# Other pauses of TensorE's side threads in a two-layer RWKV7 and latent-attention block, and a higher scheduler priority for its attention scores

## The chip, the cores and the metric

The kernel runs on one core of one Trainium2 chip. The metric is the device time of one execution in microseconds (us). Engines are named as in the profile: PE is TensorE, DVE is VectorE, ACT is ScalarE, POOL is GpSimd, SP is SyncE.

## The reference, cut to what matters

One block with two layers works on 256 tokens of width 2048. Each layer mixes tokens in two ways from one input projection, a linear-attention recurrence (RWKV7, 16 heads of 64) and a causal softmax attention with compressed keys and queries (MLA, 8 heads), then projects both together with `w_out`. A memory cross-attention and a feed-forward part (2048 to 8192 and back) follow.

```python
def rwkv7_scan(r, decay, k, v, kk, a):
    def step(state, inp):
        r_t, w_t, k_t, v_t, kk_t, b_t = inp
        sa = jnp.einsum('bhvk,bhk->bhv', state, -kk_t)
        state = (state * w_t[:, :, None, :]
                 + sa[..., :, None] * b_t[:, :, None, :]
                 + v_t[..., :, None] * k_t[:, :, None, :])
        return state, jnp.einsum('bhvk,bhk->bhv', state, r_t)
...
    if v_first is None:
        v_first = v
    else:
        vr = token_shift(vres_cols, mu_vres)
        v = v + (v_first - v) * jax.nn.sigmoid(v0 + vr @ v_up)
...
def causal_block_attention(qn, qr, kn, kr, v):
...
        s = (jnp.einsum('bqhd,bkhd->bhqk', qn[:, q0:q1], kn[:, :q1])
             + jnp.einsum('bqhr,bkr->bhqk', qr[:, q0:q1], kr[:, :q1])).astype(jnp.float32) * scale
...
        p = jax.nn.softmax(s, axis=-1).astype(v.dtype)
        outs.append(jnp.einsum('bhqk,bkhd->bqhd', p, v[:, :q1]))
```

In layer 1 the values `v` are blended with those of layer 0 (`v_first`); in layer 0 they are not. That is why one edit below depends on the layer.

## The kernel before, in words

**The main line.** All large products (called gemms here) run on PE. A weight tile of 128x1024 is loaded by SP (512 KB), rounded on ACT to a high part `wh` (L291), and the remainder `wl` is made on DVE by a subtraction (L292). Each product is done three times, as wh with the high part of the activations, wl with the high part and wh with the low part, and these PE rows all carry the line L243 (transposes L248).

**The side threads.** The small chains of each layer are Python generators, called fibers: `f_inner` (the RWKV chunk products of a group of 8 heads), `f_v` (the values), `f_qr` (rotary queries), `f_lane` (three attention heads), `f_out` (end of the recurrence) and others. Each layer has two groups, g0 and g1. PE's order is written out by the program itself (`tc.manual_schedule` for PE alone, L1522): after every step of a gemm the main line calls `poll()` (L185), which lets every fiber run whose due time has passed. The clock for this is a model, `self.clk`, which each matmul advances by an estimate. `yield x` in a fiber means: come back when this clock has moved on by x times 1.1 (`LAT`, L164). So a longer pause puts more gemm products between two steps of a fiber, and everything later in that fiber stands later in PE's order. Nothing of this clock exists on the chip: there PE takes its rows in the order written and waits for operands and buffers.

The other four engines are ordered by the Tile scheduler from program order and priorities; `high_priority(offset=300)` makes it treat the instructions inside as if they stood 300 places earlier.

**PSUM.** The fibers share four banks, given out in turn by `xps()` (tiles `x`); the gemms have four more (tiles `g`). A bank is free again only when the engine that empties it has done so.

**Where the change acts.** `f_inner` multiplies four chunks: each takes two banks and 16 small matmuls (L720, rows `x<-AR,BK`), then DVE multiplies by a mask out of the two banks (L723, `W<-x,C`, two rows), ACT copies the diagonal blocks (L725), and the fiber pauses at L728. After the fourth chunk come the bonus products (L743, `x<-prod,C`) and three rounds of transposes (L751, `x<-Id,BK`, copied by ACT at L752). The operands AR and BK are made on DVE (L688 to L696), the `prod` tiles at L701. `f_v` waits at L836 until the values `vT` are there (token shift: `yp` L496, `yd` on POOL L501, `vT` L504). In layer 1 it then blends in `v_first` (POOL's DMA at L842 and products at L843 and L844, DVE's addition L845) and pauses 6.2 (L849); then it transposes the values in two rounds of four (L854, `x<-Id,vT`, copied by ACT at L857). `f_lane` computes the scores of a head, takes the masked row maximum on DVE (L1145, L1147), the exponential on ACT (L1150) and the division by the sum on DVE (L1152, L1155), pauses 9.6, and transposes (`x<-Id,pr`). The results of the query and key gemms leave PSUM through ACT (`kn` L1109, `qn` L1115) and DVE (`vv` L1112). `f_out` ends the recurrence: normalised outputs `oc` (L953) are transposed (`x<-Id,oc`) and gated (`x<-gl,gup`), DVE makes `yo` (L964, L966), ACT its high part `oh` (L967), DVE the low part `ol` (L968), and the `w_out` gemm reads `oh` and `ol`. That gemm's rows with these operands are named `g<-wh,oh`, those with the attention's operands `mh` and `ml`. The recurrence's own chain on DVE, a long row of small pairs (L798, L800), runs beside all this.

Of the kernel before, what the change touches and what calls it, by code (L numbers as in the profile page):

```python
# [11 lines left out]
AF = mybir.ActivationFunctionType  # L12
ALU = mybir.AluOpType
# [9 lines left out]
NEG = -3.0e38  # L23
# [110 lines left out]
class K:  # L134
# [571 lines left out]
    def f_inner(self, l, g, R, prods):  # L706


        nc = self.nc
# [4 lines left out]
        for c in range(4):  # L714
            W = self.t4("W", [128, 8, 128])
            pw = [self.xps().rearrange("p (h t) -> p h t", h=4) for _ in range(2)]
            for i in range(4):
                for q in range(2):
                    rows = slice(64 * q, 64 * q + 64)
                    self.mm(pw[q][:, i, :], BK[i // 2][rows, i % 2, c].rearrange("p a b -> p (a b)"),  # L720
                            AR[i // 2][rows, i % 2, c].rearrange("p a b -> p (a b)"), True, True)
            for q in range(2):
                nc.vector.tensor_tensor(out=W[:, 4 * q : 4 * q + 4, :], in0=pw[q], in1=mw, op=ALU.mult)  # L723
            for b in range(2):
                nc.scalar.copy(out=G[b * 32 : b * 32 + 32, :, c * 8 : c * 8 + 8].rearrange("p t i -> p i t"),  # L725
                               in_=W[b * 32 : b * 32 + 32, :, b * 32 : b * 32 + 32])
            Ws.append(W)
            yield (0.1, 0.1)[g]  # L728
        N = self.t4("N", [128, 32, 32])
        nc.vector.transpose(out=N[:64].rearrange("p a b -> p (a b)"), in_=G[:64].rearrange("p a b -> p (a b)"))  # L730
        nc.vector.tensor_copy(out=N[64:], in_=N[:64])
# [15 lines left out]
        for c in range(3):  # L747
            tok = self.t2("tok", [128, 8, 64])
            ps = self.xps().rearrange("p (i t) -> p i t", i=4)
# [16 lines left out]
        for h in range(2):  # L766
            nc.gpsimd.memset(UT[64 * h + 32 : 64 * h + 64, :, :, 0:32], 0.0)
            for b in range(2):
                nc.scalar.copy(out=UT[64 * h + 32 * b : 64 * h + 32 * b + 32, :, :, 32 * b : 32 * b + 32],
                               in_=Ud[32 * b : 32 * b + 32].rearrange("p (c g j) t -> p c g j t", c=4, g=2)[:, :, h])  # L770
        yield (1.2, 1.2)[g]
        for half in range(2):
# [4 lines left out]
            for h in range(2):  # L777
                nc.scalar.copy(out=UT[64 * h : 64 * h + 32, 2 * half : 2 * half + 2, :, 32:64],
                               in_=p2[0:32].rearrange("p (c g j) t -> p c g j t", c=2, g=2)[:, :, h])
# [35 lines left out]
    def f_v(self, l, g, sm, R):  # L815
# [3 lines left out]
        if l:  # L819
# [5 lines left out]
            for b in range(2):  # L825
# [8 lines left out]
                sgs.append(sg)  # L834
                yield (1.0, 1.0)[g]
        yield ("vT", l, g)  # L836
        vT = R["vT"]
        for b in range(2):
            bs = slice(2 * b, 2 * b + 2)
# [282 lines left out]
    def f_lane(self, l, heads, M):  # L1122
        nc = self.nc
        sc = float(192.0) ** -0.5
        am = self.c("amask")
        yield ("qr", l)
        mh, ml = M["m"]
        for h in heads:
            g, i = h // 4, h % 4
            yield ("proj", l, g)  # L1130
            kn, vv, qn = M["k"][g]
            qrT, krz = M["qrT"], M["krz"]
            ps = self.xps()
            pr = self.t2("pr", [128, 384])
            mx, nm, sm, ri = (self.sm(s, [128, 2]) for s in ("mx", "nm", "sum", "ri"))
            for t in range(2):
                n = 128 * (t + 1)
                o = ps[:, t * 128 : t * 128 + n]
                ts = slice(t * 128, (t + 1) * 128)
                self.mm(o, qn[:, i, ts], kn[:, i, :n], True, False)  # L1140
                self.mm(o, qrT[:, h // 2, ts], krz[:, h % 2, :n], False, True)
            for t in range(2):
                n = 128 * (t + 1)
                o = ps[:, t * 128 : t * 128 + n]
                nc.vector.tensor_tensor_reduce(out=o, in0=o, in1=am[:, t * 128 : t * 128 + n], scale=1.0, scalar=NEG,  # L1145
                                               op0=ALU.add, op1=ALU.max, accum_out=mx[:, t : t + 1])
            nc.vector.tensor_scalar(out=nm, in0=mx, scalar1=-sc, scalar2=None, op0=ALU.mult)  # L1147
            for t in range(2):
                n = 128 * (t + 1)
                nc.scalar.activation(out=pr[:, t * 128 : t * 128 + n], in_=ps[:, t * 128 : t * 128 + n], func=AF.Exp,  # L1150
                                     scale=sc, bias=nm[:, t : t + 1], accum_out=sm[:, t : t + 1])
            nc.vector.reciprocal(out=ri, in_=sm)  # L1152
            for t in range(2):
                n = 128 * (t + 1)
                nc.vector.tensor_scalar(out=pr[:, t * 128 : t * 128 + n], in0=pr[:, t * 128 : t * 128 + n], scalar1=ri[:, t : t + 1], scalar2=None, op0=ALU.mult)  # L1155
            yield 9.6
            pt = self.xps()
            for b in range(3):
                self.tr(pt[:, b * 128 : (b + 1) * 128], pr[:, b * 128 : (b + 1) * 128])
            prT = self.t2("prT", [128, 384])  # L1160
            nc.scalar.copy(out=prT, in_=pt[:, :384])
            yield 2.0
            po = self.xps()
            vs = slice(i * 128, (i + 1) * 128)
            self.mm(po[:, 0:256], vv[:, 0, vs], prT[:, 0:256], True, False)
            self.mm(po[:, 128:256], vv[:, 1, vs], prT[:, 256:384], False, True)
            o = mh[h // 4][:, h % 4, :]
            nc.scalar.copy(out=o, in_=po[:, :256])
            nc.vector.tensor_tensor(out=ml[h // 4][:, h % 4, :], in0=po[:, :256], in1=o.bitcast(F32), op=ALU.subtract)
            self.fire(("mla", l, h), 1.5)  # L1170
            yield 0.1
# [366 lines left out]
```

## Time and profile before

| what | value |
|---|---|
| median of 3 runs | 2571.5 us (2571.23 to 2571.56) |
| profiled execution | 2572.03 us |
| its span | 2570.3 us |
| mean granted TensorE clock | 0.99 |
| PE busy | 2504.9 us (97%), so 65.4 us idle |
| DVE busy | 1655.6 us (64%) |
| ACT busy | 1211.0 us (47%) |
| POOL busy | 457.8 us (18%) |

Times in the profile count from the start of the span. A timeline row gives the start, the busy time, the engine, the line, the operation, the tiles (output, then inputs), shapes, and `x` with the number of instructions merged in it; in brackets stands how long the engine was idle before it and which instruction ended that. A row of the windows gives, for a stretch of time, the busy time and number of instructions of each engine, the clock granted to PE (PEclk, 1.00 is full), the share of DMA engines in use, and GB/s. A row of the waits gives the waiting instruction, the one that ended the waits, and how much in all, how often, and the longest.

### The profile page before, as it was taken

What the parts mean: (1) busy time and instruction counts of PE and PEld (TensorE: products, weight loads), DVE (VectorE), ACT (ScalarE), POOL (GpSimd) and SP (SyncE); (2) the same over time, 40 slices, a digit from 0 to 9 for tenths busy, and PEclk for the clock granted to TensorE, in tenths of its full rate; (3) what the DMA queues carried; (4) which work ended last, traced back from release to release, by engine and by line L of the source; (5) the groups of instructions that cost most, each with busy time, mean ns of one, the idle gap of its engine ahead of it and who ended that gap; (6) DMA issues with size and microseconds to landing.
All of it is one profiled execution on the core that took longest, in us unless ns stands there. A gap on an engine that the chain in (4) does not pass through costs nothing.

```text
span 2570.3 us, 39517 instructions
## 1 busy us (share of the span) xinstructions
PE 2504.9 (97%) x15538; PEld 2176.2 (85%) x15538; DVE 1655.6 (64%) x2245; ACT 1211.0 (47%) x1740; POOL 457.8 (18%) x609
## 2 busy tenths in 40 slices
PE   8999999999999999999999998999999999999998
PEld 7989888978888888888788987889788888888886
DVE  4776876676565566566757778656755655665665
ACT  5454555554444444444454544545544443444443
POOL 3323425221000000001124244202200000000010
PEclk9999999999999999999999999999999999999999
DMA  6555356746666666666654544565466566666664
GB/s 228 151 154 139 121 167 204 229 135 183 193 189 189 193 189 189 189 192 206 199 168 135 155 126 122 163 226 186 137 186 193 190 183 197 190 188 190 194 205 132
DMA packets 257163, 456.53 MB, mean 178 GB/s; under 512 B 25588, under 2 KB 58740, under 8 KB 256976
## 3 DMA queue, kind: packets, MB, share of 16 engines
q1 hardware_dynamic: 247600, 422.79, 53.1%
q0 software_dynamic: 9376, 31.21, 3.9%
q8 instruction: 122, 2.00, 0.3%
q14 instruction: 65, 0.53, 0.1%
HBM read 444.50 MB, written 9.44 MB: 177 GB/s over the span
## 4 chain that ended last, share of the span: by engine, by line
PE 86%; DVE 6%; POOL 2%; issue 2%; ACT 1%; DMA 1%; SPq 0%; DVEq 0%; POOLq 0%; ACTq 0%
PE g L243 52%; PE x L243 33%; DVE wl L292 2%; PE x L248 2%; DMA raw<-in_w_in_dram 1%; ACT wh L291 1%; DVE fs L798 1%; DVE T L800 0%; DVE h L485 0%; ACT junk L396 0%; DMA raw<-in_w_ff_dram 0%; DMA vf<-vfirst 0%; DVE uf L424 0%; POOL yd L501 0%; POOL rsn L647 0%
## 5 line engine op out<-in xcount | busy, mean ns | idle before, releaser
L292 DVE TENSOR_TENSOR wl<-raw,wh 128x1024 fp32r<-128x1024 f32 (+2 forms) x804 | 1009.8, 1261 | 695.7 <-ACT wh L291 693.0
L291 ACT CAST wh<-raw 128x1024 fp32r<-128x1024 f32 (+2 forms) x804 | 835.3, 1043 | 967.2 <-PE g L243 534.7
L243 PE MATMUL g<-u,wh 128*128 128x512 f32 x1024 | 362.6, 398 | 0.0
L243 PE MATMUL x<-u,wh 128*128 128x512 f32 x896 | 317.0, 398 | 0.0
L243 PE MATMUL g<-u,wl 128*128 128x256 f32 x1024 | 285.1, 281 | 0.0
L1386 POOL TENSOR_TENSOR rl<-rl 128x512 f32<-128x512 f32 x60 | 70.3, 1172 | 1153.0 <-ACT rl L1385 1153.0
L243 PE MATMUL g<-uh,wh 128*128 128x256 f32 x896 | 263.4, 294 | 0.0
L243 PE MATMUL g<-uh,wl 128*128 128x256 f32 x896 | 253.4, 283 | 0.4 <-DVE wl L292 0.4
L243 PE MATMUL g<-ul,wh 128*128 128x256 f32 x896 | 253.2, 283 | 0.0
L243 PE MATMUL x<-u,wl 128*128 128x256 f32 x896 | 248.9, 280 | 0.0
L243 PEld LDWEIGHTS g<-u,wh 128*128 128x128 f32 x1024 | 192.4, 188 | 45.7
L243 PEld LDWEIGHTS x<-u,wh 128*128 128x128 f32 x896 | 168.3, 188 | 40.7
L243 PE MATMUL g<-wl,hdh 128*128 128x512 f32 x512 | 199.4, 390 | 0.4 <-DVE wl L292 0.4
L243 PE MATMUL g<-wh,hdh 128*128 128x512 f32 x512 | 199.4, 389 | 0.0
L243 PE MATMUL g<-wh,hdl 128*128 128x512 f32 x512 | 199.2, 389 | 0.0
L243 PE MATMUL x<-wh,hdh 128*128 128x512 f32 x512 | 199.2, 389 | 0.0
L243 PE MATMUL x<-wl,hdh 128*128 128x512 f32 x512 | 199.2, 389 | 0.0
L243 PE MATMUL x<-wh,hdl 128*128 128x512 f32 x512 | 199.2, 389 | 0.0
L243 PEld LDWEIGHTS g<-u,wl 128*128 128x128 f32 x1024 | 193.5, 189 | 1.4
L243 PEld LDWEIGHTS g<-uh,wh 128*128 128x128 f32 x896 | 171.3, 191 | 4.5 <-issue 2.0
L243 PEld LDWEIGHTS g<-uh,wl 128*128 128x128 f32 x896 | 171.6, 192 | 2.6 <-issue 1.7
L243 PEld LDWEIGHTS g<-ul,wh 128*128 128x128 f32 x896 | 171.4, 191 | 0.0
(366 smaller groups left out, 4362.6 us busy)
## 6 DMA issues: line engine op xcount, KB each, us to landing
raw<-in_w_ff_dram SPq DMA_DIRECT2D x512, 512.0 KB, 4.1
raw<-in_w_in_dram SPq DMA_DIRECT2D x112, 512.0 KB, 4.1
raw<-in_w_out_dram SPq DMA_DIRECT2D x64, 512.0 KB, 3.9
raw<-in_wk_mem_dram SPq DMA_DIRECT2D x16, 512.0 KB, 4.2
raw<-in_wq_mem_dram SPq DMA_DIRECT2D x16, 512.0 KB, 3.9
raw<-in_wv_mem_dram SPq DMA_DIRECT2D x16, 512.0 KB, 4.3
raw<-in_wo_mem_dram SPq DMA_DIRECT2D x16, 512.0 KB, 3.6
raw<-in_w_in_dram SPq DMA_DIRECT2D x16, 448.0 KB, 5.8
```

The source lines that it names most:

```text
L243: return self.nc.tensor.matmul(out, lhsT, rhs, start=start, stop=stop, skip_group_check=skip)
L248: self.nc.tensor.transpose(out, in_, self.ident[p0 : p0 + n, p0 : p0 + n])
L291: nc.scalar.copy(out=wh, in_=raw)
L292: nc.vector.tensor_tensor(out=wl, in0=raw, in1=wh.bitcast(F32), op=ALU.subtract)
L798: nc.vector.tensor_tensor(out=tmp, in0=N[:, s + 1 :, s : s + 1].to_broadcast([128, m, w]), in1=T[:, s : s + 1, :w].to_broadcast([128, m, w ...
L1386: nc.gpsimd.tensor_tensor(out=r, in0=r, in1=r, op=ALU.mult)
```

## The change

Three edits, no arithmetic added or removed:

- the pause between the chunk products (L728) grows from 0.1 to 1.5, in both groups and both layers;
- in layer 0 the fiber of the values pauses 3.0 after the values are announced, where it had no pause (layer 1 keeps its 6.2);
- in `f_lane`, the maximum, the exponential and the division are issued under `high_priority(offset=300)`.

```diff
-            yield (0.1, 0.1)[g]
+            yield (1.5, 1.5)[g]
...
         yield ("vT", l, g)
+        if not l:
+            yield 3.0
         vT = R["vT"]
...
-            for t in range(2):
-                n = 128 * (t + 1)
-                o = ps[:, t * 128 : t * 128 + n]
-                nc.vector.tensor_tensor_reduce(out=o, in0=o, in1=am[:, t * 128 : t * 128 + n], scale=1.0, scalar=NEG,
-                                               op0=ALU.add, op1=ALU.max, accum_out=mx[:, t : t + 1])
-            nc.vector.tensor_scalar(out=nm, in0=mx, scalar1=-sc, scalar2=None, op0=ALU.mult)
...
+            with self.tc.high_priority(offset=300):
+                for t in range(2):
+                    n = 128 * (t + 1)
+                    o = ps[:, t * 128 : t * 128 + n]
+                    nc.vector.tensor_tensor_reduce(out=o, in0=o, in1=am[:, t * 128 : t * 128 + n], scale=1.0, scalar=NEG,
+                                                   op0=ALU.add, op1=ALU.max, accum_out=mx[:, t : t + 1])
+                nc.vector.tensor_scalar(out=nm, in0=mx, scalar1=-sc, scalar2=None, op0=ALU.mult)
...
             yield 9.6
```

Because later steps of a fiber move along, the order changes far beyond the edited lines. Three places follow; the numbers behind the names only tell one tile from another.

PE in layer 0, group 0, before. `x_1413` and `x_1414` are the two banks of the first chunk, `g_...` rows the gemm's products.

```order
L248 MATMUL x_1383<-Id,vT_1302 128x128 x4
L243 MATMUL g_1319<-wh_1329,uh_104 128x512
L243 MATMUL g_1319<-wl_1330,uh_104 128x512
L243 MATMUL g_1319<-wh_1329,ul_108 128x512
L243 MATMUL g_1320<-wh_1329,uh_104 128x512
L243 MATMUL g_1320<-wl_1330,uh_104 128x512
L243 MATMUL g_1320<-wh_1329,ul_108 128x512
L248 MATMUL x_1404<-Id,vT_1302 128x128 x4
L243 MATMUL x_1413<-AR_1152,BK_1154 128x128
L243 MATMUL x_1414<-AR_1152,BK_1154 128x128
```

The same place after: `x_1405` and `x_1406` are the first chunk, `x_1446` and `x_1447` the second.

```order
L243 MATMUL x_1405<-AR_1153,BK_1155 128x128
L243 MATMUL x_1406<-AR_1153,BK_1155 128x128
L248 MATMUL x_1425<-Id,vT_1302 128x128 x4
L243 MATMUL g_1319<-wh_1367,uh_105 128x512
L243 MATMUL g_1319<-wl_1368,uh_105 128x512
L243 MATMUL g_1319<-wh_1367,ul_109 128x512
L243 MATMUL g_1320<-wh_1367,uh_105 128x512
L243 MATMUL g_1320<-wl_1368,uh_105 128x512
L243 MATMUL g_1320<-wh_1367,ul_109 128x512
L248 MATMUL x_1438<-Id,vT_1302 128x128 x4
L243 MATMUL x_1446<-AR_1152,BK_1154 128x128
L243 MATMUL x_1447<-AR_1152,BK_1154 128x128
```

The first transposes of the values stood ahead of the first chunk and now stand behind it; 24 gemm products instead of 12 lie ahead of the pair, and 12 instead of 6 between the later chunks.

DVE in layer 1, group 1, before: from the second chunk's mask products (`W_15398`) to the fourth's (`W_15473`).

```order
L723 TENSOR_TENSOR W_15398<-x_15399,C 128x512
L723 TENSOR_TENSOR W_15398<-x_15400,C 128x512
L504 SCALAR_TENSOR_TENSOR vT_15413<-yd_15417,V,yp_15414 128x256 x2
L504 SCALAR_TENSOR_TENSOR vT_15413<-yd_15424,V,yp_15421 128x256 x2
L723 TENSOR_TENSOR W_15452<-x_15453,C 128x512
L723 TENSOR_TENSOR W_15452<-x_15454,C 128x512
L845 TENSOR_TENSOR vT_15413<-vT_15413,vf_15488 128x512
L845 TENSOR_TENSOR vT_15413<-vT_15413,vf_15493 128x512
L723 TENSOR_TENSOR W_15473<-x_15474,C 128x512
L723 TENSOR_TENSOR W_15473<-x_15475,C 128x512
```

After, from the first chunk's (`W_15422`) on; `W_15459` is the second's, `ru` and `rw` belong to the rotary queries.

```order
L723 TENSOR_TENSOR W_15422<-x_15423,C 128x512
L723 TENSOR_TENSOR W_15422<-x_15424,C 128x512
L292 TENSOR_TENSOR wl_15517<-raw_15513,wh_15516 128x1024
L847 TENSOR_TENSOR vT_15382<-vT_15382,vf_15443 128x512
L847 TENSOR_TENSOR vT_15382<-vT_15382,vf_15448 128x512
L292 TENSOR_TENSOR wl_15600<-raw_15596,wh_15599 128x1024
L723 TENSOR_TENSOR W_15459<-x_15460,C 128x512
L723 TENSOR_TENSOR W_15459<-x_15461,C 128x512
L292 TENSOR_TENSOR wl_15607<-raw_15603,wh_15606 128x1024
L292 TENSOR_TENSOR wl_15719<-raw_15715,wh_15718 128x1024
L1030 TENSOR_TENSOR ru_15494<-qrx_15492,C 128x256
L1031 TENSOR_TENSOR rw_15495<-qrx_15492,C 128x256
```

The blending of the values (L845 before, L847 after) stood behind the third chunk's mask products and now stands ahead of the second's.

PE in layer 1, the end of the recurrence, before: the last gating products and what follows them.

```order
L243 MATMUL x_16903<-gl_12472,gup_16759 128x128
L243 MATMUL x_16903<-gl_12472,gup_16760 128x128
L243 MATMUL x_16805<-wh_16888,mh_15561 128x512
L243 MATMUL x_16805<-wl_16889,mh_15561 128x512
L243 MATMUL x_16805<-wh_16888,ml_15563 128x512
L243 MATMUL x_16806<-wh_16888,mh_15561 128x512
L243 MATMUL x_16806<-wl_16889,mh_15561 128x512
L243 MATMUL x_16806<-wh_16888,ml_15563 128x512
```

The same place after, where `oh_16437` and `ol_16438` are written from these gating products (the rows of `g_16103` read their second half).

```order
L243 MATMUL x_16954<-gl_12472,gup_16849 128x128
L243 MATMUL x_16954<-gl_12472,gup_16850 128x128
L243 MATMUL g_16103<-wh_16942,oh_16437 128x512
L243 MATMUL g_16103<-wl_16943,oh_16437 128x512
L243 MATMUL g_16103<-wh_16942,ol_16438 128x512
L243 MATMUL g_16102<-wh_16942,oh_16437 128x512
L243 MATMUL g_16102<-wl_16943,oh_16437 128x512
L243 MATMUL g_16102<-wh_16942,ol_16438 128x512
```

Before, gemm rows of the attention's half stood behind the gating; now the rows that read its result stand there at once.

More of the change, by code (lines that the diff above doesn't have):

```diff
@@ L1141, in f_lane @@
                 self.mm(o, qrT[:, h // 2, ts], krz[:, h % 2, :n], False, True)
-            for t in range(2):
-                n = 128 * (t + 1)
-                o = ps[:, t * 128 : t * 128 + n]
-                nc.vector.tensor_tensor_reduce(out=o, in0=o, in1=am[:, t * 128 : t * 128 + n], scale=1.0, scalar=NEG,
-                                               op0=ALU.add, op1=ALU.max, accum_out=mx[:, t : t + 1])
-            nc.vector.tensor_scalar(out=nm, in0=mx, scalar1=-sc, scalar2=None, op0=ALU.mult)
[L1148 to L1155, printed above, removed]
+            with self.tc.high_priority(offset=300):
[5 more added lines that the diff above has]
+                nc.vector.tensor_scalar(out=nm, in0=mx, scalar1=-sc, scalar2=None, op0=ALU.mult)
+                for t in range(2):
+                    n = 128 * (t + 1)
+                    nc.scalar.activation(out=pr[:, t * 128 : t * 128 + n], in_=ps[:, t * 128 : t * 128 + n], func=AF.Exp,
+                                         scale=sc, bias=nm[:, t : t + 1], accum_out=sm[:, t : t + 1])
+                nc.vector.reciprocal(out=ri, in_=sm)
+                for t in range(2):
+                    n = 128 * (t + 1)
+                    nc.vector.tensor_scalar(out=pr[:, t * 128 : t * 128 + n], in0=pr[:, t * 128 : t * 128 + n], scalar1=ri[:, t : t + 1], scalar2=None, op0=ALU.mult)
             yield 9.6
```

## The prediction

> **What bounds the kernel now.** I read the busy times first, then the waits of PE, then the clock in windows around each wait, and last the timelines at these places.
>
> ```profile
> PE 2504.9 (97%) x15538; PEld 2176.2 (85%) x15538; DVE 1655.6 (64%) x2245; ACT 1211.0 (47%) x1740; POOL 457.8 (18%) x609
> ```
>
> PE is the bound: 2504.9 of 2570.3 us are busy. No matmul goes away, so the change can win only idle time of PE (65.4 us) and time at a lower clock. The waits of PE over the whole run (total, times, longest) name what it idles for at the edited places, and the second answer does so for layer 1, group 1 and the attention behind it alone:
>
> ```profile
> PE x L243 <- DVE W L723: 5.9, 3, 3.9
> PE g L243 <- ACT wh L291: 5.7, 5, 3.2
> PE g L243 <- ACT qn L1115: 5.3, 2, 2.8
> PE x L248 <- DVE vT L504: 4.6, 4, 2.4
> ```
>
> ```profile
> PE g L243 <- ACT qn L1115: 2.4, 1, 2.4
> PE x L248 <- POOL qr L1030: 1.9, 1, 1.9
> PE x L248 <- DVE W L723: 1.6, 1, 1.6
> PE x L243 <- DVE W L723: 1.1, 1, 1.1
> PE g L243 <- ACT qrx L1091: 1.1, 1, 1.1
> PE x L248 <- ACT tok L752: 1.0, 1, 1.0
> ```
>
> Behind the waits the granted clock falls to half (columns: us, busy time and count of PE, PEld, DVE, ACT, POOL, then PEclk):
>
> ```profile
> 121.50:128.40 6.90, 6.42 (x29) 4.82 (x29) 6.57 (x14) 3.37 (x5) 3.11 (x9) 0.51 0.26 83
> 278.50:285.40 6.90, 6.73 (x38) 5.67 (x39) 5.61 (x8) 4.07 (x8) 0.24 (x2) 0.51 0.79 229
> 322.90:326.30 3.40, 3.40 (x13) 2.81 (x12) 3.23 (x9) 2.50 (x4) 1.36 (x3) 0.50 0.91 300
> 1408.40:1415.20 6.80, 6.18 (x29) 5.33 (x30) 5.92 (x8) 5.43 (x9) 0.00 (x1) 0.50 0.48 125
> 1585.80:1589.20 3.40, 3.40 (x14) 2.92 (x13) 2.99 (x13) 1.83 (x3) 0.98 (x2) 0.51 0.68 210
> 1606.30:1609.70 3.40, 3.12 (x8) 2.44 (x9) 3.19 (x13) 2.60 (x4) 2.77 (x6) 0.50 0.83 275
> ```
>
> Six stretches of 3.4 or 6.9 us run at half clock with PE almost fully busy, so each costs half its length: 1.7 or 3.4 us. Priced whole, idle and clock together, the places are: layer 0 group 0, 2.2 (three of the four vT waits, 4.6 − 2.4) + 3.4 = 5.6; layer 0 group 1, 2.4 + 3.4 = 5.8; layer 0 attention, 2.8 + 1.7 = 4.5; layer 1 group 0, 3.9 and 0.9 (5.9 − 3.9 − 1.1) + 3.4 = 8.2; layer 1 group 1, 1.6 + 1.1 + 1.1 + 1.0 + 1.9 = 6.7, + 1.7 = 8.4; layer 1 attention, 2.4 + 1.7 = 4.1. Together 36.6 us: the most that the change can win here.
>
> **The change part by part.** What a longer pause buys is gemm work between two steps, to cover a wait. Its worth per product:
>
> ```profile
> 414.27 4.10 PE g L243 x18
> ```
>
> ```profile
> 1325.46 43.18 PE g L243 x360
> ```
>
> That is 0.23 us for a product 512 wide and 0.12 us for one 256 wide. The gemm products come from the same main line, so they are not added but taken from later. Where a half-clock stretch stands behind a wait that shrinks but stays, I charge half of what keeping it or losing it would make, and keep both ends.
>
> *Layer 0, group 0.* In the new order 24 products instead of 12 stand ahead, then the first chunk c0, the first value transposes, 6 products, the second transposes, c1. DVE's queue there is nearly unchanged:
>
> ```profile
> 124.20 0.41 DVE L696 TENSOR_TENSOR BK<-kT,en 128x256 f32<-128x256 f32 x1
> 124.54 1.26 DVE L701 SCALAR_TENSOR_TENSOR prod<-rT,V,kT 128x256 f32<-128x256 f32 x3
> 125.73 2.34 DVE L292 TENSOR_TENSOR wl<-raw,wh 128x1024 fp32r<-128x1024 f32 x2
> 128.70 1.29 DVE L723 TENSOR_TENSOR W<-x,C 128x512 f32<-128x512 f32 x2 [0.62 <-PE x L243]
> ```
>
> ```profile
> 130.18 1.16 PE L243 MATMUL x<-AR,BK 64*128 64x128 f32 x16
> ```
>
> The last BK is ready at 124.6, so c0, now earlier in PE's order, waits for it. W of c0 comes behind the prods and the two wl: 125.7 + 2.3 + 1.3 = 129.4, and c1 needs the two banks that W empties (the transposes took the other two). So c1 starts at 129.4 instead of 130.18, with 6 more products done (1.4): −2.1 at full clock. At half clock the 3.7 us of PE work between 124.6 and 129.4 (c0 1.2, transposes, 6 products 1.4) takes 7.4 and c1 comes at 132: +0.5. Taken: **−0.8**.
>
> *Layer 0, group 1.* c0 stands some 24 products (2.9) earlier, and DVE makes the values behind c0 and c1 instead of ahead of them.
>
> ```profile
> 271.25 0.41 DVE L696 TENSOR_TENSOR BK<-kT,en 128x256 f32<-128x256 f32 x1
> 271.58 1.26 DVE L701 SCALAR_TENSOR_TENSOR prod<-rT,V,kT 128x256 f32<-128x256 f32 x3
> 272.77 1.27 DVE L496 TENSOR_TENSOR yp<-g,rbc 128x512 f32<-128x512 f32 x2
> 274.60 2.43 DVE L504 SCALAR_TENSOR_TENSOR vT<-yd,V,yp 128x256 f32<-128x256 f32 x4 [0.55 <-POOL yd L501]
> ```
>
> ```profile
> 288.65 1.03 PE L243 MATMUL x<-prod,C 128*128 128x256 f32 x4
> ```
>
> Two weight subtractions fewer stand ahead of the last BK (2 × 1.17), so it comes at about 269.0 instead of 271.25. From there DVE's row in the new order is prods 1.6, seven wl 8.2, yp 1.2, vT 2.4 and the eight W, 4.5 up to the first half of the last: 269.0 + 17.9 = 286.9, when the bonus products get their bank. Before they started at 288.65, and by then 12 products more (1.4) will be done: 1.75 + 1.4 = −3.1. The half-clock stretch of 3.4 that stood here is inside that, and new waits of PE (about 2 for BK, 1 for W) can keep 1.7 of it: −1.4. Taken: **−2.3**. If DVE is not 2 us earlier this term is nothing; if PE's waits vanish with the clock it is −5.8.
>
> *Layer 0, attention.* In DVE's new order the row maxima stand ahead of four small chain rows (0.3 each) more than before, and the third head's exponential moves with them; behind it ACT has a weight cast and then the qn copy for which PE waits.
>
> ```profile
> 312.02 0.28 DVE L798 TENSOR_TENSOR fs<-N,T 128x126 f32<-128x126 f32 x1
> ```
>
> ```profile
> 321.61 1.07 ACT L1115 COPY qn<-g 128x512 f32<-128x512 f32 x2
> ```
>
> ```profile
> 324.42 1.48 PE L248 MATMUL x<-Id,pr 128*128 128x128 f32 x6
> ```
>
> I put that copy 0.8 earlier, an estimate between nothing and the 1.2 of those rows. The six probability transposes, 1.5 at half clock and so about 1.0 at full, now stand ahead of the waiting gemm, inside the wait: 1.8 of the 2.8 goes. Half of the 1.7 behind it: **−2.7** (−1.8 to −4.5).
>
> *Layer 1, group 0.* The order is c0, 12 products, c1, 12, c2, value transposes, 6, transposes, c3; it was c0, 6, c1, 6, c2, 6, c3.
>
> ```profile
> 1409.02 2.67 PE L243 MATMUL x<-AR,BK 64*128 64x128 f32 x16 [3.90 <-DVE W L723]
> ```
>
> What came to c3 at 1409.0, the bank that W of c1 empties, now serves the transposes, one wl (1.1) later: 1410.1, because POOL's blending, which holds DVE's queue, has not moved. Up to c2 PE has 12 products more but 6 fewer behind it, and no 0.9 wait: it reaches the transposes at 1405.1 + 1.4 − 0.9 = 1405.6 and idles 4.5 instead of 4.8. Half of a shorter stretch: **−1.0** (−0.3 to −1.8).
>
> *Layer 1, group 1, up to the scores.* The longer pauses push the value transposes behind c2, ahead of the product that took their place. Behind `yp` comes a fixed path: yd on POOL, the DMA of v_first, two blends, DVE's addition.
>
> ```profile
> 1555.81 2.04 POOL L501 TENSOR_TENSOR yd<-yp 128x512 f32<-128x512 f32 x2 [6.68 <-DVE yp L496]
> 1557.79 1.19 POOL L842 DMA_DIRECT2D vf<-vfirst  x2
> ...
> 1562.11 1.28 POOL L843 TENSOR_TENSOR vf<-vf,vT 128x512 f32<-128x512 f32 x1 [2.26 <-DMA vf<-vfirst]
> ```
>
> ```profile
> 1550.37 1.16 PE L243 MATMUL x<-AR,BK 64*128 64x128 f32 x16
> ```
>
> From yp on: half of yp 0.6, yd 2.0, the DMA until the first blend 4.3, four POOL products of 1.3 (5.1), DVE's addition 0.7, one wl 1.2, half of W 0.65, together 14.5 to the bank. An estimate puts yp at 1554, straight behind the prods, whose chain has moved later: the bank is free at 1568.5. PE starts c0 2.8 later than 1550.4 (12 products of 0.12 and 6 of 0.23), and with c0 to c2 (3 × 1.1) and 5.5 of gemm reaches the transposes at 1562.1: idle 6.4. c3 then waits for W of c2, behind the rest of W 0.65, two wl 2.3, five rotary rows of 0.4 and 1.3 of its own, 6.3, against 2.8 of PE work: 3.5. The 6.7 of waits go in exchange, since the qr rows come earlier and the later ones have cover. 9.9 − 6.7 − 1.7 = +1.5; a stretch behind the new long wait makes it +3.2. Taken: **+2.3**. This is the most uncertain term; with yp at 1552 the wait is 4.4, at 1557 it is 9.4.
>
> *Layer 1, attention.* Here most transposes and a second batch of scores stand between the qn copy and the `w_out` gemm, so the whole 2.4 and the stretch of 1.7 go: **−4.1**; if the clock falls anyway, −2.4.
>
> *Layer 1, end of the recurrence.* Gemm rows that covered the last gating are gone: PE waits for yo, oh and ol.
>
> ```profile
> 1688.81 0.69 DVE L966 TENSOR_TENSOR yo<-yo,x 128x512 f32<-128x512 f32 x1 [0.20 <-PE x L243]
> 1690.19 0.69 DVE L968 TENSOR_TENSOR ol<-yo,oh 128x512 fp32r<-128x512 f32 x1 [0.69 <-ACT oh L967]
> ```
>
> oh is done when ol can start, 1.4 after yo's start; that is the wait, then 0.2 for oc and 0.3 more for ol behind two products: +1.9, half a short stretch (0.85) on top: **+2.7**.
>
> Sum: −0.8 − 2.3 − 2.7 − 1.0 + 2.3 − 4.1 + 2.7 = **−5.9**. The profiled execution of 2572.03 would take 2566.1; it lies 0.5 above the median, so I forecast a median of **2565.6**. With all stretches gone: −2.1 − 3.1 − 3.5 − 1.8 + 1.5 − 4.1 + 1.9 = −11.2; with all kept: +0.5 − 1.4 − 1.8 − 0.3 + 3.2 − 2.4 + 3.6 = +1.4. The forecast's own range is 2560.3 to 2572.9.
>
> On the clock, a row speaks against counting stretches this way for certain: the one from 121.5 follows three idles of 2.2 together, while the one from 1408.4 follows 3.9 in one piece. The Trainium skill (TensorE: Matmul & The Clock Gate, "HAM oscillation — how this bites in real kernels") puts the danger at idle gaps of more than about 3.4 us; of the six stretches here only that from 1408.4 follows such a gap, so the trace disagrees with it as a full account.
>
> **The rivals.** *A: the cover is enough.* The gemm work put between the steps outlasts DVE's queue, waits and stretches go together. For it: in four of the six places DVE's own rows are short beside 12 products (2.7). Against: DVE's rows stand back to back at the three places above, and the new order puts wl ahead of W. Of the 36.6 at most half seems open: 2571.5 − 18.3 = 2553.2.
>
> *B, slower: DVE's queue in group 1 is the bound in both layers.* Place: prods and yp. If BK in layer 0 comes no earlier than now and yp in layer 1 at 1557 instead of 1554, group 1 of layer 0 gains nothing (0), layer 1's wait becomes 9.4 + 3.5 + 3.4 − 8.4 = +7.9, its attention is late with it (0), the tail pays 3.6: −0.8 + 0 − 2.7 − 1.0 + 7.9 + 0 + 3.6 = +7.0, so 2578.5. It passes +5.1 at a yp of 1555.1. For it: rope rows and wl stand ahead of W; against: the values' rows moved ahead in DVE's queue.
>
> *C: only single gaps longer than a window drop the clock.* Then short waits that go leave the stretches where they are, and the one new gap of 6.9 adds 1.7: the terms become +1.3, +0.3, −1.8, −0.3, +4.9, −2.4, +1.9, together +3.9: 2575.4. This is what the rule of the Trainium skill named above would make of the change. Only one stretch of six fits it.
>
> *D: the change does nothing here.* Moved waits are replaced by equal ones: 2571.5.
>
> **How the numbers follow.** About 0.2%, 5.1 us, is what a measurement of this kernel can tell from no change. Forecast 0.48, of which 0.30 lies beyond −5.1 and 0.18 within it; A 0.24, all faster; B 0.16, slower; C 0.07 and D 0.05, within. So faster 0.54, same 0.30, slower 0.16. The range reaches from A's value to B's, 2553 to 2578.5, which leaves out half of each, 0.20.
>
> **What would show it.** In the new profile: PE's waits for vT L504 near 120 and 276 gone, c0 there waiting for BK instead; the qn waits near 1606 gone and near 322 about 1 us; a new wait of 5 to 10 us at the value transposes of layer 1, group 1, near 1562; a wait of 1.4 for oh at the end of the recurrence. Wrong if that new wait is missing (then A), or if half-clock stretches stand as before (then C). The sum is wrong in kind if gains come from places not named here.

## The result, and the profile after

The changed kernel takes 2595.7 us (median, 2590.9 to 2597.6) against 2571.4 for the kernel before on the same chip. The ratio is 1.0093, with a 95% interval of 1.0079 to 1.0106: slower by about 24 us. The forecast was 2565.6, and its range ended at 2578.5. The time lies outside, on the other side. One execution behind this document, of e13, was in a slow state (2762.77 us at a mean clock of 0.844), and no median below counts it.

The profiled execution took 2590.94 us, with a span of 2589.2; it is the fastest of the four (the others took 2594.87 to 2597.62), so some 5 us of the loss are not in it. The busy times of its page:

```profile
PE 2504.7 (97%) x15538; PEld 2178.4 (84%) x15538; DVE 1657.4 (64%) x2245; ACT 1211.3 (47%) x1740; POOL 454.9 (18%) x609
```

PE is as busy as before (2504.7 against 2504.9 us), and the span is 18.9 us longer. In these two executions the whole difference is idle time of PE: 84.5 us instead of 65.4. Added up from the timeline, layer 0 has 12.5 us of it (10.6 before, 23.1 after) and layer 1 7.4 (16.9 and 24.3). The waits of PE over the whole run (in all, times, longest) say for what:

```profile
PE g L243 <- DVE wl L292: 13.6, 13, 2.6
PE x L248 <- DVE W L723: 8.2, 2, 5.6
PE x L243 <- ACT sq L637: 8.1, 2, 6.5
PE x L243 <- ACT prT L1164: 5.5, 1, 5.5
...
PE g L243 <- DVE vv L1114: 3.2, 3, 1.4
PE x L243 <- DVE W L723: 3.0, 2, 2.0
PE g L243 <- ACT oh L969: 2.2, 1, 2.2
```

The waits that the change was read to remove are gone: vT (4.6 before) has no row, and qn (5.3 before) is down to one of 0.6. Two others have come that the prediction does not name, `sq` with 8.1 and `prT` with 5.5. The wait for `wl` has grown from 7.7 to 13.6, in 13 pieces. The two new ones belong to fibers that the diff does not touch: `sq` is the first step of the next group, `prT` the transposed probabilities of an attention head.

**Where sq comes from.** The chain of waits in the window from 236 to 249, in parts (start, duration, what):

```profile
235.91 0.41 ACT VS L914
...
237.31 1.21 ACT junk L396 x5
...
240.00 0.55 POOL rsq L255
240.55 0.64 POOL gup L928
...
241.80 1.11 POOL ru L1030
242.91 0.21 POOL rw L1031
243.12 0.53 POOL gup L928
...
246.90 0.22 POOL krt L1032
...
247.15 0.52 ACT sq L637
```

The timeline of PE at its end, and of ACT (idle time before the row and its releaser in brackets):

```profile
240.52 0.68 PE L243 MATMUL x<-X,UT 64*64 64x64 f32 x16
247.71 0.59 PE L243 MATMUL x<-C,sq 128*128 128x2 f32 x2 [6.51 <-ACT sq L637]
```

```profile
235.91 0.83 ACT L914 COPY VS<-Sn 64x256 f32<-64x256 f32 x2 [2.83 <-DVE Sn L910]
...
247.15 0.51 ACT L637 ACTIVATE sq<-kT,V 128x256 f32<-128x256 f32 x1 [6.01 <-POOL krt L1032]
```

PE stands 6.5 us before the first product of group 1. It waits for ACT, ACT for POOL, and POOL works off its queue: norms, two DMA issues and the rotary key (`ru`, `rw`, `krt`). The norms need squares made on ACT (`junk`), and in ACT's queue these stand behind the copies of the state of group 0's recurrence (`VS` from `Sn`), for which ACT waited 2.83 us. The rotary key has nothing to do with `sq`, except that both take their buffers from one ring of eight (`self.t1`). That ring also holds the recurrence's tiles `X` and `Sn`. In the kernel before the same rotary rows ran on POOL from 223 to 229, and `sq` waited for no one but its own input:

```profile
228.99 0.25 POOL L1030 TENSOR_TENSOR krt<-ru,rw 128x32 f32<-128x32 f32 x1
```

```profile
237.87 1.76 ACT L637 ACTIVATE sq<-kT,V 128x256 f32<-128x256 f32 x4 [1.35 <-DVE kT L504]
```

**Where prT comes from.** All engines near 340, after:

```profile
339.46 0.17 DVE L800 TENSOR_TENSOR T<-T,fs 128x16 f32<-128x16 f32 x1
...
339.72 0.65 ACT L806 COPY Tb<-T 64x512 f32<-64x512 f32 x1 [3.99 <-DVE T L800]
340.27 0.46 ACT L1164 COPY prT<-x 128x384 f32<-128x384 f32 x1
...
340.79 0.79 PE L243 MATMUL x<-prT,vv 128*128 128x256 f32 x1 [5.46 <-ACT prT L1164]
```

In ACT's queue the copy `Tb` stands ahead of the copy `prT`. `Tb` waits 4.0 us for the last row of the serial chain on DVE; `prT`, whose input was there, waits behind it. Before, the third `prT` copy stood ahead of `Tb`:

```profile
328.58 0.47 ACT L1161 COPY prT<-x 128x384 f32<-128x384 f32 x1
...
330.61 0.67 ACT L806 COPY Tb<-T 64x512 f32<-64x512 f32 x1 [0.29 <-DVE T L800]
```

The chain ends 9.0 us later than before (339.6 and 330.6). More than half of that is PE itself running late: the third head's transposes ran at 327.38 before and run at 332.14 now. Against them the chain is 4.3 us late.

The clock in windows (columns as above, PEclk after the five engines): the first three are places named in the prediction, the others new stretches.

```profile
121.50:128.40 6.90, 5.21 (x32) 3.85 (x31) 6.90 (x15) 1.75 (x3) 3.34 (x10) 0.84 0.25 79
278.50:285.40 6.90, 6.90 (x66) 6.51 (x66) 6.90 (x11) 2.68 (x4) 0.00 (x0) 1.00 0.29 83
1606.30:1609.70 3.40, 3.40 (x22) 2.96 (x21) 3.12 (x10) 0.00 (x0) 1.57 (x4) 1.00 0.59 161
125.50:129.75 4.25, 4.25 (x22) 3.27 (x23) 4.25 (x7) 1.37 (x3) 0.00 (x0) 0.60 0.33 79
245.35:256.40 11.05, 8.69 (x44) 8.55 (x46) 1.02 (x3) 3.95 (x8) 5.53 (x11) 0.54 0.52 105
337.15:344.80 7.65, 4.01 (x13) 3.54 (x14) 6.69 (x17) 1.38 (x3) 1.58 (x1) 0.55 0.55 186
```

The stretches at 278.5 and 1606.3 are gone as forecast. New ones stand at the two new waits, so in sum nothing is won at the clock (mean granted clock 0.990 before and 0.988 after).

### The profile page after: what moved, and what is told of

It reads as the page before. It is cut to its first block, busy times and chain, and to the rows that moved or that the text cites. A ratio compares the mean times of both kernels' runs of the same rounds, so it can differ in the third digit from the quotient of the medians.

```text
span 2589.2 us, 39515 instructions
## 1 busy us (share of the span) xinstructions
PE 2504.7 (97%) x15538; PEld 2178.4 (84%) x15538; DVE 1657.4 (64%) x2245; ACT 1211.3 (47%) x1740; POOL 454.9 (18%) x609
## 4 chain that ended last, share of the span: by engine, by line
PE 82%; DVE 9%; POOL 3%; issue 3%; ACT 2%; DMA 1%; SPq 0%; DVEq 0%; POOLq 0%; ACTq 0%
PE g L243 49%; PE x L243 32%; DVE wl L292 2%; PE x L248 1%; DVE fs L798 1%; DVE T L800 1%; ACT wh L291 1%; DMA raw<-in_w_in_dram 1%; DVE h L485 0%; DVE W L723 0%; DMA raw<-in_w_ff_dram 0%; ACT junk L396 0%; DVE uf L424 0%; DMA vf<-vfirst 0%; POOL yd L501 0%
```

## The experiments

All ratios are to the kernel before on the same chip (its medians were 2570.0 to 2571.5). Letters stand for theories as each expectation words them.

| run | what it is | median us | ratio, 95% |
|---|---|---|---|
| e1 | pause edit alone | 2597.3 | 1.0099 (1.0085 to 1.0113) |
| e2 | the other two edits alone | 2571.4 | 0.9999 (0.9990 to 1.0007) |
| e3 | changed kernel, rotary key in rings of its own | 2585.0 | 1.0054 (1.0042 to 1.0067) |
| e4 | changed kernel, `Tb` copied on DVE | 2596.5 | 1.0097 (1.0082 to 1.0113) |
| e5 | changed kernel, pause in group 0 only | 2593.2 | 1.0085 (1.0072 to 1.0099) |
| e6 | changed kernel, pause in group 1 only | 2594.5 | 1.0084 (1.0070 to 1.0098) |
| e7 | e3 with `Tb` on DVE and `ml` on POOL | 2589.7 | 1.0068 (1.0056 to 1.0081) |
| e8 | e5 with the rings of e3 | 2583.5 | 1.0046 (1.0033 to 1.0058) |
| e9 | e5, recurrence of group 0 put back | 2575.0 | 1.0014 (1.0005 to 1.0023) |
| e10 | e6, recurrence of group 1 put forward | 2585.4 | 1.0054 (1.0038 to 1.0071) |
| e11 | changed kernel, both recurrences put forward | 2590.7 | 1.0076 (1.0061 to 1.0091) |
| e12 | kernel before with the rings of e3 | 2571.4 | 1.0000 (0.9991 to 1.0010) |
| e13 | kernel before, recurrence of group 0 later | 2592.7 | 1.0081 (1.0064 to 1.0098) |
| e14 | kernel before, recurrence of group 1 later | 2586.6 | 1.0063 (1.0046 to 1.0080) |
| e15 | changed kernel, pause 0.8 instead of 1.5 | 2582.3 | 1.0045 (1.0030 to 1.0060) |

### Which edit: e1 and e2

e1 is the kernel before with only the first edit, e2 the changed kernel without it.

```diff
-            yield (0.1, 0.1)[g]
+            yield (1.5, 1.5)[g]
```

> The changed kernel with the longer pause between the chunk products alone: no pause of the values, no raised priority. Theory P (the pause between the chunk products makes the whole loss, the other two edits move only a few instructions): 2592 to 2599 us, slower than before by 0.8 to 1.1%, with the waits of the changed kernel for sq (6.5 us near 247) and for prT (5.5 us near 341) in it. Rival Q (the loss comes from the pause of the values or from the priority together with it): within 5 us of before, 2571 to 2577 us.

> The pause of the values and the priority, with the pause between the chunk products left at 0.1. Theory P: 2567 to 2574 us, no difference that can be measured or a small gain; no wait for sq or prT of more than 1 us. Rival Q: slower than before by over 10 us.

The pause alone gives the whole loss (2597.3), with both new waits (`sq` 6.5, `prT` 5.3 the longest). The pause of the values and the priority together change nothing that can be measured: in e2 the vT waits are gone, but waits for `W` have grown from 5.9 to 10.8 us in their place.

### Is it the two waits: e3, e4, e7

e3 gives the rotary key's tiles buffers of their own; PE's order stays that of the changed kernel.

```diff
-            u = self.t1("ru", [128, n, 32])
+                u = self.tp.tile([128, n, 32], F32, tag="kr1", name=self.nm("ru"), bufs=8)
...
-            krt = self.t1("krt", [128, 2, 64])
+            krt = self.tp.tile([128, 2, 64], F32, tag="kr2", name=self.nm("krt"), bufs=2)
```

> The changed kernel with buffers of their own for the small tiles of the rotary keys (ru, rw, krt), which otherwise share a ring of eight buffers with the squares sq and with the recurrence's tiles X and Sn. The order of PE is the same; on POOL the rotary keys move ahead. Theory S (sq waits because its buffers are held by the rotary keys, and these wait for the recurrence of group 0, which the longer pauses moved later): the wait for sq of 6.5 us goes, with most of the half-clock stretch behind it (5.1 us), so 2583 to 2590 us against 2596 of the changed kernel. Rival T (the small chains are late as a whole and the next late wait takes over): sq's wait is replaced by another at the same place, 2593 to 2597 us.

10.7 us come back. The timeline of ACT in e3 shows the four squares in one piece, with no wait, 7 us earlier, and PE's rows at `C,sq` follow at 241.0 without one:

```profile
239.97 1.70 ACT L637 ACTIVATE sq<-kT,V 128x256 f32<-128x256 f32 x4
```

```profile
241.01 1.95 PE L243 MATMUL x<-C,sq 128*128 128x2 f32 x16
```

The scheduler now puts the rotary rows much earlier in POOL's queue: they run from 169.8 to 176.0, not from 241.8. So the ring is shown to be the cause of this wait. e12, below, shows that the rings are no gain in themselves. The wait for `prT` is untouched (5.45): there the chain ends at 333.7, only 3.1 later than before, and the third head's transposes run at 326.24, so the chain is again 4.2 late against them.

e4 takes `Tb` out of ACT's queue.

```diff
-        nc.scalar.copy(out=Tp[:, 1], in_=Th[64:])
+        nc.vector.tensor_copy(out=Tp[:, 1], in_=Th[64:])
```

> The changed kernel with the second copy of the inverse (Tb, line 806) on DVE instead of ACT; the order of PE is the same. Theory S (that copy waits on ACT for the long DVE chain and holds up the third head's prT behind it, for which PE waits 5.5 us, with a half-clock stretch of 3.4 us behind): 2586 to 2592 us against 2596 of the changed kernel, and PE's wait for prT gone. Rival T: PE waits as long at the next place, 2593 to 2597 us.

That was wrong. The waits of PE in e4:

```profile
PE x L243 <- DVE ml L1172: 4.0, 1, 4.0
PE x L243 <- ACT prT L1164: 0.8, 1, 0.8
```

The wait for `prT` shrinks from 5.5 to 0.8, and the next step of the same head, `ml` on DVE behind the same serial chain, takes 4.0. The kernel is as slow as the changed one.

e7 then frees both: own rings, `Tb` on DVE, and `ml` subtracted on POOL from a copy in SBUF that ACT makes in addition.

```diff
+            oc = prT[:, 0:256]
+            nc.scalar.copy(out=oc, in_=po[:, :256])
+            nc.scalar.copy(out=o, in_=oc)
+            nc.gpsimd.tensor_tensor(out=ml[h // 4][:, h % 4, :], in0=oc, in1=o.bitcast(F32), op=ALU.subtract)
```

> The changed kernel with three moves: own buffers for the rotary keys (as in the run with the own ring), the second Tb copy on DVE, and the low part ml of the attention's output made on POOL from a copy in SBUF that ACT makes (one ACT copy of 128x256 more for each head), so that the PSUM bank no longer waits for DVE. Theory V (PE's wait at the third head is for the end of the long DVE chain, which reaches it on whichever engine's queue it stands in: prT behind Tb on ACT, ml behind the chain on DVE): both waits gone, 2575 to 2582 us against 2585 with the own ring alone. Rival T (the next wait takes over): 2583 to 2588 us.

It is 4.7 us slower than e3, outside both ranges. `prT` still waits 1.6, and `pr` (1.2) and `M` (2.0) are new. Taking away the wait that the profile names did not give its time back twice in a row; it was time to ask what made the chain late.

### Which group: e5, e6, e8

The pause is (1.5, 0.1) in e5 and (0.1, 1.5) in e6; e8 is e5 with the rings of e3.

> The changed kernel with the longer pause in group 0 alone (group 1 back at 0.1). Theory S (group 0's pauses delay its recurrence, which holds the ring of eight buffers that group 1's squares need): the wait for sq of 6.5 us near 247 stays, the wait for prT near 341 goes, since on ACT the third prT now stands ahead of Tb; 2580 to 2588 us. Rival U (the loss is made in group 1, by its own pauses): 2570 to 2576 us.

> The changed kernel with the longer pause in group 1 alone (group 0 back at 0.1). Theory S: no wait for sq, and on ACT the prT copies stand ahead of Tb, so that only what layer 1's group 1 loses is left: 2571 to 2580 us. Rival U: 2588 us or more.

> The longer pause in group 0 alone, with own buffers for the rotary keys. Theory S: without the wait for sq the longer pause of group 0 costs nothing: 2568 to 2575 us, no difference to before or a small gain. Rival: the pause costs by itself, through the later recurrence of group 0: 2578 us or more.

Each group alone costs 22.1 and 23.5 us, and both together 24.3: the parts don't add. In e5 `sq` waits 6.5 as in the changed kernel; the expectation for the rest of the loss was missed, because a wait stands where the changed kernel has none, at the end of layer 0. The timeline of PE in e5, and in e8:

```profile
417.17 1.09 PE L248 MATMUL x<-Id,oc 128*128 128x128 f32 x4 [7.12 <-DVE oc L955]
```

```profile
412.05 1.09 PE L248 MATMUL x<-Id,oc 128*128 128x128 f32 x4 [7.12 <-DVE oc L955]
```

e8 wins 9.7 us by the rings and still waits the same 7.12 for `oc`, the output of the recurrence. So its rival held in the number: the pause has a price of its own. But the row that waits belongs to group 1, and in the order it stands 2.7 us of gemm earlier than before, not later; what it waits for is a collision on POOL: the norm that it needs (`rs`, `grs`, 412.8 to 416.3 in e5) has three products of the memory (`mem`, 1.6 us each) ahead of it or between its two rows, where before all four were over at 396.4 and the norm ran from 398.1 to 400.0. In e6 there is no wait for `sq` at all, and yet the gemm product that ran at 453.3 before runs 20.0 us late: this expectation was missed too. Rival U fails as well, since it gave e5 no loss. PE's busy time from 385 to 440 (first number behind the comma), before, after and in e6:

```profile
385.00:440.00 55.00, 55.00 (x332) 45.40 (x332) 35.73 (x49) 30.62 (x55) 27.20 (x23) 1.00 0.53 175
```

```profile
385.00:440.00 55.00, 55.00 (x377) 45.34 (x375) 34.89 (x54) 27.36 (x45) 22.14 (x23) 1.00 0.55 181
```

```profile
385.00:440.00 55.00, 43.78 (x336) 35.16 (x335) 28.62 (x54) 23.18 (x43) 29.38 (x28) 0.91 0.39 130
```

### Is it the chunk products or the recurrence: e9 to e15

A longer pause moves two things: the chunk products of its group, and behind them the recurrence (`Tr,W`, `Sn,AR`, `Id,oc`). Counted by the gemm products ahead of each row, with the prices of the prediction, the changed kernel has the recurrence of group 0 up to 5.8 us later in both layers and that of group 1 5.5 to 11 later in layer 1, but in layer 0 1.4 earlier. A number of the program separates them: `f_fs` yields `FSD` × 4 seven times between the chunk products and the recurrence. One fifth of that (0.2 × 4 × 7 × 1.1 = 6.2) is what four pauses of 1.4 add (4 × 1.4 × 1.1 = 6.2). Theory F says that the recurrence costs, rival K that the chunk products do. e9 has the pause in group 0 without the later recurrence, e13 the later recurrence without the pause.

```diff
-                yield self.FSD[g] * self.FS
+                yield self.FSD[g] * self.FS * (1.0 if g else 0.8)
```

> Inner pauses (1.5, 0.1) as in the run with the pause in group 0 alone (2593.2), and the pace of the serial rows f_fs of group 0 cut by a fifth (0.8 instead of 1.0), which takes 6.2 off the model clock, as much as the four pauses add. In the order, the chunk products of group 0 stay late (+1.4 to +4.1 us of gemm) but its recurrence (Tr,W, Sn,AR, Id,oc) stands again exactly where it stood before, in both layers. Theory F, the loss comes from the recurrence that is moved, not from the chunk products: in layer 0 the wait for sq (6.5 us in the run with the pause in group 0) and the wait for oc at 417 (7.1) go, layer 0 ends within 3 us of before instead of 18 late, whole kernel 2568 to 2578. Rival K, the chunk products' own new places cost it (waits for W and wl, half clock beside them): 2588 or more.

e13 has 1.2 there instead of 0.8, in the kernel before, with its pause of 0.1.

> The kernel before with one number changed: the pace of the serial rows f_fs of group 0 raised by a fifth (1.2 instead of 1.0). Pauses, chunk products of group 0 and priorities as before; in the order the recurrence of group 0 stands 7 to 9 us of gemm later. Theory F, the recurrence that is moved is the cost: the waits of the pause in group 0 come back without any longer pause, sq near 248 (5 to 8 us) and oc near 417, whole kernel 2583 to 2598. Rival K, the chunk products' new places are the cost: 2568 to 2575.

Both fall as F had it: 2575.0 and 2592.7. PE's busy time from 225 to 275, the place of the `sq` wait, in the order before, after, e9, e13:

```profile
225.00:275.00 50.00, 47.83 (x475) 45.62 (x474) 42.55 (x84) 26.82 (x56) 29.78 (x45) 1.00 0.44 117
```

```profile
225.00:275.00 50.00, 40.56 (x399) 38.57 (x394) 33.69 (x72) 20.91 (x48) 26.64 (x46) 0.90 0.30 75
```

```profile
225.00:275.00 50.00, 49.30 (x486) 46.98 (x485) 43.12 (x85) 26.83 (x56) 29.69 (x45) 1.00 0.43 117
```

```profile
225.00:275.00 50.00, 40.95 (x390) 38.58 (x386) 34.03 (x72) 19.37 (x45) 26.81 (x46) 0.84 0.28 77
```

With the recurrence put back the place is as full as before, pauses or not; with it moved the 7 us are missing, and the clock is 0.84 to 0.90, though no chunk product of that group was moved in e13. In group 0 the recurrence's place is the cause, and not the chunk products of that group: undoing it takes back 18 of 22 us, and doing it alone costs 23 us. It is the place with all that hangs on it: in e13, as in e5, the chunk products of group 1 stand up to 5.8 us of gemm earlier. In e13 the wait of 6.5 for `sq` stands in layer 1; in layer 0 the rotary key is late in another row, with 4.4 for `krt` at 242, which the expectation did not have.

> Inner pauses (0.1, 1.5) as in the run with the pause in group 1 alone (2594.5), and the pace of f_fs of group 1 cut by a fifth. Chunk products of group 1 stay late; its recurrence stands 4.1 us of gemm earlier than before in layer 0 and 2.7 earlier in layer 1. Theory F: the +17 us at the end of layer 0 goes; because the serial rows on DVE cannot be quicker than they are (32 us in layer 0), PE may wait up to 4 us for Tr near 340 and 1620: 2570 to 2580. Rival K: 2588 or more.

> The same in group 1: f_fs of group 1 at 1.2, so its recurrence stands 4 to 5.5 us of gemm later in layer 0 and 7 to 10 later in layer 1, and every chunk product and value transpose stands where it stood. Theory F: layer 0 ends 10 us or more late, with waits at its last gatings near 410 to 430, as in the run with the pause in group 1 alone; whole kernel 2581 to 2596. Rival K: 2568 to 2575.

> The changed kernel with the pace of f_fs cut by a fifth in both groups, the shared ring of buffers as it is. The order puts the recurrence of group 0 where it stood before, that of group 1 4.1 earlier in layer 0 and 4.1 later in layer 1. Theory F: no wait for sq in group 1 (krt and the others get their buffers as before), wait for prT 2 us or less, whole kernel 2570 to 2582, with what is left in layer 1 group 1. Rival K: 2588 or more.

In group 1 the later recurrence, with every chunk product where it stood (e14), costs 16.6 us, most of it at layer 0's end: PE is busy 44.92 of the 55 us there, and waits for `mem`, `oc` and `oh`:

```profile
428.78 1.11 PE L248 MATMUL x<-Id,mem 128*128 128x128 f32 x4 [4.80 <-POOL mem L1186]
```

The order shows why this longest wait is one for `mem`: a third fiber has moved. Most of the memory's transposes stand 13.7 us of gemm earlier in e14 and 17.8 earlier in e6 (which waits 5.19 there). In the changed kernel they stand where they stood, or 1.4 earlier, and PE is busy without a break from 385 to 440. So e6 and e14 show that the order at layer 0's end is sensitive, but not what group 1 costs in the changed kernel.

But putting it forward (e10) brought only 9 of 23 us back, less than expected, and with both groups (e11) 5 of 24, a miss of F's upper end by 9 us. The timeline of PE in e10 shows the reason in layer 0:

```profile
342.29 3.59 PE L243 MATMUL x<-Tr,W 32*32 32x32 f32 x64 [4.74 <-DVE Tr L811]
```

`Tr` is made at the end of DVE's serial chain, which runs from 298.6 to 333.6 there (298.0 to 330.6 before) and starts only when the fourth chunk is there. PE's order can be put earlier, that chain can't: PE then waits at `Tr,W` itself. e11 waits 8.7 us for `Tr` in two places and 14.6 for `W` at the value transposes. These last stand between the moved chunk products, so K is not nothing; the time is in K's range.

> The changed kernel with inner pauses of 0.8 instead of 1.5. In the order the chunk products and the value transposes move in nearly the same way (12 products instead of 6 between some of them), the recurrence by no more than 1.4 in three of the four places and 4.1 in layer 1 group 1. Theory F: most of the loss goes, 2569 to 2580. Rival K: 2585 or more.

With half the pause the recurrence starts (`Tr,W`) at most 1.4 later in three of the four places, and 12 of the 24 us are gone. The rest is more than F allowed. Its waits are those of the moved chunk products and of the attention, one of each from its timeline:

```profile
284.19 1.12 PE L248 MATMUL x<-Id,vT 128*128 128x128 f32 x4 [4.67 <-DVE W L723]
```

```profile
1623.64 1.65 PE L243 MATMUL x<-prT,vv 128*128 128x256 f32 x4 [5.71 <-ACT prT L1164]
```

> The kernel before with the rotary key tiles in rings of their own, the edit that won 10.7 us on the changed kernel. Theory S, the shared ring costs only where the recurrence is late: nothing, 2569 to 2574. Rival: the extra buffers are a gain in themselves: 2562 or less.

The control gives no change: the ring costs only where the recurrence is late.

What is shown: the loss comes from the pause edit (e1, e2); 10.7 of its 24 us come through the ring, with PE's order unchanged (e3, e12); and with the pause in group 0 alone, 18 of 22 us hang on where the recurrence of group 0 stands (e9, e13). What stays open: how the other 14 us of the changed kernel divide. The wait for `prT` is in it; e5, without group 1's pauses, does not have that wait, which points to the late fourth chunk of group 1, but no run moved that chunk alone. No run put the recurrence of group 0 alone back in the changed kernel: e11, which puts back both, has group 1's in layer 0 4.1 earlier than before. Open too is why the groups don't add. In the order, a late group 0 moves group 1's recurrence the other way (5.5 earlier at its start in e5), which would explain it; that was not tried. No version beats the kernel before.

## Why the prediction was wrong, point by point

The gemm products of the main line come in the same order in both kernels, so a stage can be priced by how much later one and the same product runs at its end. The products of this table are such that the same small rows stand ahead of them before and after (e3 has the order of the changed kernel).

| product that ran before at (us), at the end of | later in the changed kernel | later in e3 | predicted for the stage |
|---|---|---|---|
| 183.8: layer 0, group 0 | 1.2 | 1.1 | −0.8 |
| 299.7: `sq` and layer 0, group 1 | 7.8 | 1.5 | −2.3 |
| 385.0: layer 0, attention | 13.1 | 7.4 | −2.7 |
| 1388.8: up to layer 1's chunk products | 12.5 | 6.7 | 0 |
| 1437.4: layer 1, group 0 | 13.0 | 7.2 | −1.0 |
| 1704.1: layer 1, group 1, attention, end of the recurrence | 18.9 | 12.6 | +0.9 |

- **PE as the bound, a gain only from its idle time and clock**: right, and the loss came the same way.
- **Layer 0, group 0 (−0.8)**: right at the place, and yet no gain. c0 waits 1.69 for BK at 124.9 instead of for vT; but PE then waits for `wl` at 155.3 and 159.1 (1.60 and 1.79; before, once 1.24), and the stage ends 1.2 late.
- **Layer 0, group 1 (−2.3)**: right in kind at its own places. The vT wait (2.45) and the half-clock stretch went; one new wait of 1.0 for `W` stands at 297.8. The wait for `sq` ahead of it, with the half clock behind, makes the stage a loss of 6.6; with the rings of e3 it comes out at +0.4.
- **Layer 0, attention (−2.7)**: the wait for qn fell to 0.59, as said. The step was judged at the edited wait alone; the `prT` wait 10 us behind it (5.46, with a half-clock stretch) took more than was won: +5.3. e4 shows that this is DVE's serial chain, late against the third head, and not one bad row in a queue.
- **Layer 1, group 0 (−1.0)**: the wait predicted at 4.5 came at the place named, with 5.57 us: slightly a loss (+0.5) instead of a gain.
- **Layer 1, group 1 (+2.3)**: the wait at the value transposes was 2.65 instead of 6.4, at c3 1.98 instead of 3.5. A wait of 2.60 for `wl` and two more short half-clock stretches came in their place.
- **Layer 1, attention (−4.1)**: right at the place; qn and its stretch are gone. Two waits for `vv` (1.43 and 1.05, near 1615) are new there.
- **Layer 1, end of the recurrence (+2.7)**: right, 2.95 with no stretch behind it. The waits are 2.24 for `oh` and 0.71 for `oc`.

The rows of PE in the changed kernel behind the last four points: the value transposes of layer 1 group 0, three waits of group 1, and the end of the recurrence.

```profile
1422.66 1.11 PE L248 MATMUL x<-Id,vT 128*128 128x128 f32 x4 [5.57 <-DVE W L723]
...
1573.44 0.79 PE L243 MATMUL g<-wl,qTh 128*128 128x512 f32 x1 [2.60 <-DVE wl L292]
1584.23 1.11 PE L248 MATMUL x<-Id,vT 128*128 128x128 f32 x4 [2.65 <-DVE W L723]
1590.47 1.86 PE L243 MATMUL x<-AR,BK 64*128 64x128 f32 x13 [1.98 <-DVE W L723]
...
1709.91 0.63 PE L248 MATMUL x<-Id,oc 128*128 128x128 f32 x4 [0.71 <-DVE oc L955]
1714.57 0.50 PE L243 MATMUL g<-wh,oh 128*128 128x512 f32 x1 [2.24 <-ACT oh L969]
```

The bracket is the wait and what ended it: 5.57 where 4.5 was said, 2.65 where 6.4 was, and at the end 0.71 + 2.24 where 1.9 was.

**The step that failed** is the one ahead of the list: "The gemm products come from the same main line, so they are not added but taken from later." That is right for PE's work, and the sum took it to mean that what stands later costs nothing unless it was edited. It priced the recurrence once, at the very end of layer 1. But the recurrence of group 0 moved along with the pauses, up to 5.8 us of gemm in both layers, and it shares a ring of eight buffers with the next group's first step. In the changed kernel that is the wait of 6.5 us at `sq` and the half clock behind it, a stage of +6.6 where the sum had −2.3; own rings alone take 10.7 of the 24 us back. The second term at nothing is `prT`: the chain on DVE comes 4.3 us later against the third head, PE waits 5.46, and the attention of layer 0 costs 5.3 where the sum had −2.7. The last stage of layer 1 costs 5.9 instead of 0.9; how it divides stays open. Two signs could be read ahead of the result: the rotary rows' new place on POOL, and `X` and `sq` from the same `t1`.

Rival B had the right sign and the wrong place: DVE's queue at the value transposes was no worse than in the sum. Of rival C, the clock: the stretch at 125.5 of the changed kernel follows a single idle of 1.69, that at 245.4 includes one of 6.51, and where the waits went (278.5, 1606.3) the clock stayed full, against C's condition. The Trainium skill (TensorE: Matmul & The Clock Gate, "HAM oscillation — how this bites in real kernels") names gaps of more than about 3.4 us as the danger; the trace agrees at 245.4 and disagrees at 125.5.

## What to carry to other kernels

A pause in one coroutine of a hand-written order moves everything that this coroutine does later, and steps of other coroutines the other way: list each moved step of every fiber, and for each ask which ring of buffers it shares with another fiber, what stands behind it in every in-order queue, and how much slack its consumer had. Move the step and its tail apart, by a second knob, before blaming either. And when a removed wait comes back at the next step of the same chain twice in a row, look for what made the chain late.

## What the runs showed of the hardware that was not expected

The same 15538 matmuls were busy 2514.0 us in e13 and 2504.9 in the kernel before: in e13, whose profile shows more half-clock stretches, the same work was busy 9.1 us longer, and the busy share (97% in both) doesn't show it. In the changed kernel it was not (2504.7). The busy times of e13:

```profile
PE 2514.0 (97%) x15538; PEld 2187.6 (84%) x15538; DVE 1657.9 (64%) x2245; ACT 1212.1 (47%) x1740; POOL 449.9 (17%) x609
```

Small rows on POOL are slow beside their size: in the chain at 240, the power of a single column (`rsq`) took 0.55 us, twice as long as a product of 32 columns (`rw` at 246.15, 0.24), and the issue of a DMA (`gup`) 0.64, and the rotary key waited behind both.
